# Opening weight units in places of their own, no split on GpSimd, and a reordered first norm, in a two-layer transformer block

## The chip, the cores and the metric

The kernel runs on one core of one Trainium2 chip. Its time is the device time of one execution in microseconds (us). Engines are named as in the profile: PE is TensorE's matmul, PEld its weight load, DVE VectorE, ACT ScalarE, POOL GpSimd, SP SyncE, which only issues DMAs here.

## The reference

The input is x (512 tokens, 1024 features), a context of 256 tokens, and vectors c and c_ctx that are turned into shifts, scales and gates (`w_mod`). Two layers follow, each of three sublayers, all of the form x + gate * f(modulate(rms_norm(x))):

```python
def modulate(x, g, shift, scale):
    return rms_norm(x, g) * (1.0 + scale) + shift
def macaron_half_ffn(x, g, shift, scale, gate, w_in, w_out):
    return x + 0.5 * gate * swiglu(modulate(x, g, shift, scale), w_in, w_out)
# layer 0: half FFN, even_mixer (neighbourhood attention + two-way mLSTM), half FFN
# layer 1: half FFN, spatial_gating, half FFN; then rms_norm(x, final_g)
```

In layer 0 the context goes through the first half FFN too, and feeds the mixer. An FFN is 1024 -> 2 x 2816 -> 1024. All is fp32.

## The kernel before, in words

Features lie on the partitions: x is `xT`, [128, 8, 512], the context `cT`, [128, 8, 256]. A product in fp32 accuracy is three matmuls of split operands: hi*hi, hi*lo, lo*hi (`product`; `product2` does x and context with the same weights). So each weight unit (512 KB, [128, 1024]) and each activation is split in two: ACT rounds it to `hi`, then a subtraction makes `lo = raw - hi`.

`Stream` (L61) brings the weights in one fixed order. `load` starts a DMA on SP into one of three `raw` places. `prep` splits a unit into the next of four `whi` and four `wlo` places (L81 to L84): the rounding on ACT (L83), the subtraction on DVE, or on GpSimd for the unit numbers in `W.pool` (L84). `next` hands a unit out, after splitting up to two units ahead of it and starting loads five ahead. A place of `whi` comes free when the last product with the unit in it is done. `W.pool` holds units 0 to 5, and for each of the five places in the stream where a sublayer begins (`mark`) the four units before and the four after it.

The sublayers are named by layer and number: 00 (FFN with context), 01 (mixer), 02 (FFN), 10 (FFN), 11 (gating), 12 (FFN). Each ends in `out_last` (L349): with its last four units, all held to the end, it forms the output first for tokens 0 to 255 and then for 256 to 511 (after 00 also for the context). Each of the eight products of such a part is followed by a residual on DVE (`xT`, L306), a square on ACT (`sq_x`) and an add on DVE (`nacc_x`, L230), which form the next norm's sum of squares. While the second part runs, the first part's norm is finished (`rstd`: matmul `st_x`, root on ACT, matmul `bc_x`) and DVE and ACT make the modulated input of the next sublayer, split in two (`nt_x` L255, `hx..h` L256, `hx..l` L257). The next sublayer then opens with products on tokens 0 to 255 alone, during which the second part's norm is finished. Its first four units, which hold the first weights, can be split only as `out_last` gives its four places free.

Order on each engine: a planner at build time runs through the program by its own costs, takes on each engine the ready instruction that the program names first, and so fixes each engine's queue; on the chip each engine keeps that order. Tiles whose places follow each other wait for each other's readers.

`Stage.open` (L376) reserves a sublayer's input `hx` (and `hc`) on the left side of SBUF. `gtiles` (L447) reserves the activations of an FFN, in 8 rotating places (6 with context); the last four (f 18 to 21) have places of their own, and small unused tiles (`spacer`, L44) shift some addresses by 64 or 192 bytes.

At the start of the program there is no sublayer before. x, the first modulation weights and the first weights are loaded by SP, interleaved by hand. `load_mod` (L566) loads a slice of 128 shift and 128 scale columns as four DMAs of 256 KB, whose runs are 512 bytes. `norm_start` (L589) squares on ACT, adds on DVE, and finishes the norm with matmuls (`sts`, `bcx`). `start` (L627) then goes over the eight feature blocks k: `x_products(k)` (matmuls `st`), `mod_columns(k+2)` and `mod_products(k+3)` (matmuls `pm`, a copy `mr` on DVE, matmuls `pcol`, from which DVE makes G and S of a block and then its input). The context's norm is started before block 4; its modulation and products (`stc`) follow at the end.

Of the kernel before, what the change touches and what calls it, by code (L numbers as in the profile page):

```python
# [8 lines left out]
F32 = mybir.dt.float32  # L9
F32R = mybir.dt.float32r  # L10
# [27 lines left out]
def block_kernel(ctx: ExitStack, tc: tile.TileContext, T: dict, out: bass.AP, stop: str = ""):  # L38
# [4 lines left out]
    def spacer(pool, n, name):  # L43

        nc.gpsimd.memset(pool.tile([P, n // 4], F32, name=name), 0.0)
# [15 lines left out]
    class Stream:  # L61
        def __init__(self):
            self.aps, self.raw, self.split = [], {}, {}
            self.nraw = self.nsplit = self.pos = 0
            self.pool = set()

        def load(self, upto):
# [8 lines left out]
        def prep(self, upto):  # L76
            while self.nsplit < min(upto, len(self.aps)):
                i = self.nsplit
                self.load(i + 1)
                r = self.raw.pop(i)  # L80
                hi = wp.tile(list(r.shape), F32R, tag="whi", name=f"whi{i}", bufs=4)  # L81
                lo = wp.tile(list(r.shape), F32R, tag="wlo", name=f"wlo{i}", bufs=4)
                nc.scalar.copy(hi, r)  # L83
                (nc.gpsimd if i in self.pool else nc.vector).tensor_tensor(lo, r, hi.bitcast(F32), ALU.subtract)  # L84
                self.split[i] = (hi, lo)
                self.nsplit += 1
# [262 lines left out]
    def out_last(nm, gs, gx, st, gc=None):  # L349

        u = [W.next() for _ in range(4)]
        warm(AF.Sqrt, gs[-1][1][:, 0:1].bitcast(F32))
        parts = [(xT, 0, t0, t1, gx, st.nx) for t0, t1 in HALVES]
        if gc is not None:
            parts.append((cTt[0], 2, 0, NCX, gc, st.nc))
        for x, g0, t0, t1, gg, nn in parts:
            for ot in range(KD):
                po = bank(f"pl{nm}{g0}{ot}{t0}")
                for e, g in enumerate(gs):
                    w = pick(u[ot // 2], slice(None), e, slice((ot % 2) * P, (ot % 2 + 1) * P))  # L360
                    product(po[:, :256], w, pick(g[g0:g0 + 2], slice(None), slice(t0, t1)), e == 0, e == len(gs) - 1)
                if ot in (1, 3):
                    st.go()
                residual(x, ot, t0, t1, po[:, :256], gg)
                nn.square(ot, t0, t1)
            st.feed(nn, t0, t1)


    class Stage:
# [7 lines left out]
        def open(self):  # L377
            self.stack = ExitStack()
            hp = self.stack.enter_context(tc.tile_pool(name=f"hp{self.name}", bufs=1, side=self.side, reuse_waits="tile"))
            if self.nc:  # L380
                spacer(hp, 64, f"padc{self.name}")
                self.hc = hpair(hp, NCX, f"hc{self.name}")
            spacer(hp, 64 if self.nc else 128, f"padx{self.name}")
            self.hx = hpair(hp, N, f"hx{self.name}")
            if self.name != "00":
                self.gx = gains(self.l, self.j, 0)
                self.gc = gains(self.l, self.j, 1) if self.nc else None

        def feed(self, nn, t0, t1):

# [7 lines left out]

        def close(self):
            self.stack.close()  # L400

    class Final:
        def __init__(self):
# [27 lines left out]
    def ffn(l, s, cur, nxt, gxf, gcf, bgsteps, side, first=None, left=0):  # L431
# [5 lines left out]
        with tc.tile_pool(name=f"g{nm}", bufs=1, side=side, reuse_waits="tile") as gp:  # L437
# [7 lines left out]
                    pace[0] = last  # L445

            def gtiles(f):  # L447
                e = f % nslot if hc or f < 18 else f"z{f}"
                if not hc and f == 18:
                    spacer(gp, 192, f"padz{nm}")  # L450
                g = [gp.tile([P, 512], F32R, tag=f"gx{e}{i}", name=f"gx{nm}{f}{i}") for i in range(2)]
                if hc:
                    if f < nslot:
                        spacer(gp, 192, f"padgc{f}")
                    g += [gp.tile([P, 256], F32R, tag=f"gc{e}{i}", name=f"gc{nm}{f}{i}") for i in range(2)]
                    if f < nslot:
                        spacer(gp, 64, f"padge{f}")
                if not hc and f == NF - 1:
                    spacer(gp, 64, f"padze{nm}")
                return g  # L460

            gs = {f: gtiles(f) for f in range(2)}
# [7 lines left out]
            for t0, t1 in () if first else HALVES:  # L470
                for f in range(2):
                    pab = bank(f"pa{nm}{f}{t0}"), bank(f"pb{nm}{f}{t0}")
                    for k in range(KD):
                        if (t0, f) == (0, 0) and k in (5, 7):
                            cur.go()
                        for ab in range(2):
                            w = pick(us[f][k // 4], slice(None), k % 4, slice(ab * P, (ab + 1) * P))
                            product(pab[ab][:, :256], w, pick(hx, slice(None), k, slice(t0, t1)), k == 0, k == 7)
                    glu(pab[0][:, :256], pab[1][:, :256], 256, gs[f][0][:, t0:t1], gs[f][1][:, t0:t1], f"{nm}{f}{t0}")
            bg.step(2 * bgsteps)  # L480
            for kind, f in ffn_order(l, s):
                if kind == "o":
# [64 lines left out]
    mark.append(len(W.aps))  # L547
    stream_ffn(1, 1)
    W.pool.update(range(6))
    for i in mark:  # L550
        W.pool.update(range(i - 4, i + 4))


    cpool = ExitStack()
# [12 lines left out]
    def load_mod(i):  # L567
        k0, k1 = MODK[i]
        t = sp.tile([P, KD, 2, (k1 - k0) * P], F32, tag="wmk", name=f"wmk{i}", bufs=5)
        for h in range(2):  # L570
            for j in range(2):
                nc.sync.dma_start(t[:, 4 * h:4 * h + 4, j], T["w_mod"][0, 512 * h:512 * h + 512, j * D + k0 * P:j * D + k1 * P]
                                  .rearrange("(k p) c -> p k c", p=P))
        wmk.append(t)

    for k in range(0, KD, 2):
# [9 lines left out]
        load_mod(i)  # L586
    warm(AF.Sqrt, cs[:, 0, 0:1])

    def norm_start(nn, n):  # L589
        st = aux(f"sts{n}")  # L590
        acc = sp.tile([P, N], F32, tag="sacc", name=f"sacc{n}", bufs=1)[:, :n]
        for k in range(KD):
            sq = sp.tile([P, N], F32, tag="ssq", name=f"ssq{n}{k}", bufs=4)[:, :n] if k else acc
            nc.scalar.activation(sq, nn.x[:, k], AF.Square)
            if k:
                nc.vector.tensor_tensor(acc, acc, sq, ALU.add)
        for c in range(n // P):
            mm(st[:, 2 * c:2 * c + 2], acc[:, c * P:(c + 1) * P], ones, True, True)
        r = tp.tile([P, 8], F32, tag="nrs", name=f"nrs{n}", bufs=1)[:, :n // 64]
        nc.scalar.activation(r, st[:, :n // 64], AF.Sqrt, bias=epst, scale=1.0 / D)  # L600
        if n == NCX:
            warm(AF.Silu, r[:, 0:1])
        nc.vector.reciprocal(r, r)
        bc = aux(f"bcx{n}")
        for c in range(n // P):
            mm(bc[:, c * P:(c + 1) * P], r[:, 2 * c:2 * c + 1].to_broadcast([P, P]), ident, True, True)
        return bc[:, :n]
# [12 lines left out]
    for k in range(5):  # L620
        mm(junk, ones[:, 0:1].to_broadcast([P, P]), xT[:, k], True, True)
    mrs = {0: mod_products(0)}
    bcx = norm_start(s00.nx, N)
    xn = sp.tile([P, KD, N], F32, name="xn")
    s00.open()

    def start():  # L627
# [52 lines left out]
        mod_columns(1, mrs[1])  # L680
        mrs[2] = mod_products(2)
        for k in range(KD):
            if k == 4:
                bc = norm_start(s00.nc, NCX)
            x_products(k)
            if k + 2 < KD:
                mod_columns(k + 2, mrs[k + 2])
            if k + 3 < KD:
                mrs[k + 3] = mod_products(k + 3)
# [109 lines left out]
    for cc in ((2, 3), (4, 5), (0, 1)):  # L799
        tok_block("vb0", 256, cc, ev_vb0, u01[0])  # L800
        tok_block("vb1", 272, cc, ev_vb1, u01[1])


    li = gt[:, :, 0]
# [417 lines left out]
    with tc.tile_pool(name="sgv", bufs=1, side="right", reuse_waits="tile") as vp:  # L1222
# [7 lines left out]
        for b in range(4):  # L1230
            pv = [bank(f"sv{b}{c}") for c in range(4)]
            us = [W.next() for _ in range(4)] if b == 0 else None
            for c0, c1 in ((0, 2), (2, 4)) if b == 0 else ((0, 4),):
                for i in range(4):
                    u = us[i] if b == 0 else W.next()
                    if b == c0 == 0 and i in (1, 2):
                        s11.go()
                    for c in range(c0, c1):
                        for kk in range(2):
                            k = 2 * i + kk  # L1240
                            product(pv[c], pick(hx, slice(None), k, slice(c * P, (c + 1) * P)), pick(u, slice(None), kk), k == 0, k == 7)
                for c in range(c0, c1):
                    nc.scalar.activation(halved(v[c][:, b * 512:(b + 1) * 512]), inorder(pv[c]), AF.Gelu_apprx_tanh)
        us = {}

        def ublock(b):
# [72 lines left out]
def layout(i):  # L1319
# [2 lines left out]
    a["cT"] = i["ctx"][0].T.reshape(KD, P, NCX).transpose(1, 0, 2)  # L1322
    a["cc"] = np.stack([i["c"][0], i["c_ctx"]]).reshape(2, KD, P).transpose(2, 0, 1)
    a["w_mod"] = i["w_mod"]
    a["b_mod"] = i["b_mod"].reshape(2, 9, KD, P).transpose(3, 0, 1, 2)
    a["norm_g"] = i["norm_g"].reshape(2, 3, KD, P).transpose(3, 0, 1, 2)
    a["final_g"] = i["final_g"].reshape(KD, P).T
# [74 lines left out]
```

## Time and profile before

| | |
|---|---|
| time, median of 3 runs (lowest to highest) | 2307.08 us (2306.27 to 2308.08) |
| the profiled execution's own time | 2307.41 us |
| its span, first to last instruction | 2305.6 us |
| PE busy | 2246.3 us (97%) |
| DVE busy | 1284.2 us (56%) |
| ACT busy | 779.7 us (34%) |
| POOL busy | 262.8 us (11%) |
| mean granted clock of TensorE | 0.985 |

A row of instructions has start, duration, engine, line, operation, output<-inputs with shapes, how many (x3), and in brackets the idle time of its engine just before it with what ended that. Matmuls overlap: their durations add up to more than the time they take. Where several like instructions are merged in a row, its duration is that of all of them together.

### The profile page before, as it was taken

Reading aid. Unit: us, or ns where it says so; the run is one execution under the profiler, and the core shown is the slowest. Engines: PE = TensorE matmul, PEld = TensorE weight load, DVE = VectorE, ACT = ScalarE, POOL = GpSimd, SP = SyncE. Lnnn points to the kernel's source line nnn. Section 1 sums busy time; section 2 is a strip of 40 time slices with the busy share of each in tenths; the row PEclk is TensorE's granted clock in tenths of the full one; section 3 lists DMA queues with packets and bytes.
Section 4 is the critical chain, followed back from the end, with each engine's and each line's share of the span. In section 5 each row is a group of like instructions: output and inputs, shape, how many; then the busy total and the mean of one; then the engine's idle time right before and its main releaser. Section 6 shows DMA issues by size and latency. Waiting matters only on the chain.

```text
span 2305.6 us, 31899 instructions
## 1 busy us (share of the span) xinstructions
PE 2246.3 (97%) x12926; PEld 1989.7 (86%) x12926; DVE 1284.2 (56%) x2045; ACT 779.7 (34%) x1283; POOL 262.8 (11%) x300
## 2 busy tenths in 40 slices
PE   7999999999999999999999999999999999999998
PEld 4999999999878977888888898888878888988887
DVE  5996653327556447766574766433536756433336
ACT  3322122124354356532323432322335424323222
POOL 2212120002030033100010301000300003000000
PEclk8999999999999989999999999999999999999999
DMA  8566561221122231165564356333242322333231
GB/s 268 175 201 196 167 185 65 70 68 52 63 83 65 65 119 62 65 210 192 173 211 155 111 174 210 101 101 101 92 146 93 99 92 74 101 100 108 94 110 65
DMA packets 95347, 281.33 MB, mean 122 GB/s; under 512 B 11024, under 2 KB 29632, under 8 KB 94816
## 3 DMA queue, kind: packets, MB, share of 16 engines
q1 hardware_dynamic: 69648, 196.18, 25.7%
q0 software_dynamic: 22960, 77.99, 11.3%
q10 hardware_dynamic: 2592, 5.13, 0.7%
q8 instruction: 101, 1.65, 0.3%
q14 instruction: 46, 0.38, 0.1%
HBM read 274.95 MB, written 6.00 MB: 122 GB/s over the span
## 4 chain that ended last, share of the span: by engine, by line
PE 88%; DVE 6%; issue 3%; ACT 1%; DMA 1%; POOL 0%; ACTq 0%; DVEq 0%; POOLq 0%
PE pa L108 19%; PE pb L108 19%; PE po L108 14%; PE pc L108 4%; PE su L108 4%; PE sv L108 4%; PE posg L108 3%; PE poc L108 2%; PE O L108 1%; PE tva L108 1%; PE nS L108 1%; PE st L108 1%; PE pomx L108 1%; PE fqa L108 1%; PE pl11l L108 1%
## 5 line engine op out<-in xcount | busy, mean ns | idle before, releaser
L83 ACT CAST whi<-raw 128x1024 fp32r<-128x1024 f32 x348 | 364.8, 1049 | 919.1 <-PE pb L108 330.4
L84 DVE TENSOR_TENSOR wlo<-raw,whi 128x1024 fp32r<-128x1024 f32 x302 | 370.1, 1226 | 399.6 <-ACT whi L83 383.7
L108 PE MATMUL po<-gx,whi 128*128 128x512 f32 x1024 | 305.4, 380 | 0.0
L441 DVE TENSOR_TENSOR sl<-sl,pb 128x512 f32<-128x512 f32 (+1 forms) x92 | 60.0, 652 | 272.0 <-PE pb L108 182.1
L108 PEld LDWEIGHTS po<-gx,whi 128*128 128x128 f32 x1024 | 183.7, 189 | 24.0
L108 PE MATMUL po<-gx,wlo 128*128 128x512 f32 x512 | 194.4, 380 | 0.0
L84 POOL TENSOR_TENSOR wlo<-raw,whi 128x1024 fp32r<-128x1024 f32 (+1 forms) x46 | 109.8, 2388 | 598.7 <-ACT whi L83 585.1
L161 DVE SCALAR_TENSOR_TENSOR macc<-wm,cs,macc 128x1024 f32<-128x1024 f32 x133 | 168.3, 1280 | 10.5 <-DMA wm<-in_w_mod 9.4
L153 POOL DMA_DIRECT2D wm<-in_w_mod x128 | 68.1, 532 | 573.9 <-DVE macc L161 368.7
L306 DVE SCALAR_TENSOR_TENSOR xT<-po,gate,xT 128x512 f32<-128x512 f32 x80 | 59.8, 748 | 95.9 <-PE po L108 95.8
L440 ACT ACTIVATE sl<-pa 128x512 f32<-128x512 f32 (+1 forms) x92 | 52.3, 569 | 174.3 <-PE pa L108 174.3
L108 PEld LDWEIGHTS po<-gx,wlo 128*128 128x128 f32 x512 | 97.2, 190 | 10.2
L108 PE MATMUL pc<-hc00l,whi 128*128 128x256 f32 x320 | 88.0, 275 | 0.0
L108 PE MATMUL pc<-hc00h,whi 128*128 128x256 f32 x320 | 87.3, 273 | 0.0
L108 PE MATMUL pc<-hc00h,wlo 128*128 128x256 f32 x320 | 87.2, 273 | 0.0
L108 PE MATMUL pa<-hx12l,whi 128*128 128x512 f32 (+1 forms) x192 | 70.5, 367 | 3.1 <-DVE hx12l L257 3.1
L108 PE MATMUL pa<-hx10l,whi 128*128 128x512 f32 (+1 forms) x192 | 70.2, 366 | 3.1 <-DVE hx10l L257 3.1
L108 PE MATMUL pa<-hx02l,whi 128*128 128x512 f32 (+1 forms) x192 | 70.2, 366 | 2.8 <-DVE hx02l L257 2.8
L108 PE MATMUL pa<-hx02h,whi 128*128 128x512 f32 (+1 forms) x192 | 70.3, 366 | 0.1
L108 PE MATMUL pa<-hx12h,whi 128*128 128x512 f32 (+1 forms) x192 | 70.3, 366 | 0.0
L108 PE MATMUL pa<-hx10h,whi 128*128 128x512 f32 (+1 forms) x192 | 70.1, 365 | 0.0
L108 PE MATMUL pa<-hx12h,wlo 128*128 128x512 f32 (+1 forms) x192 | 70.0, 365 | 0.0
(561 smaller groups left out, 5893.6 us busy)
## 6 DMA issues: line engine op xcount, KB each, us to landing
raw<-in_ffn_in SPq DMA_DIRECT2D x176, 512.0 KB, 3.3
wm<-in_w_mod POOLq DMA_DIRECT2D x128, 512.0 KB, 4.6
raw<-in_ffn_out SPq DMA_DIRECT2D x64, 512.0 KB, 3.3
raw<-in_mix_in SPq DMA_DIRECT2D x26, 512.0 KB, 3.2
wmk<-in_w_mod SPq DMA_DIRECT2D x32, 256.0 KB, 5.4
raw<-in_ffn_last SPq DMA_DIRECT2D x16, 512.0 KB, 3.3
raw<-in_sg_v SPq DMA_DIRECT2D x16, 512.0 KB, 3.4
raw<-in_sg_u SPq DMA_DIRECT2D x16, 512.0 KB, 3.5
```

The source lines that it names most:

```text
L83: nc.scalar.copy(hi, r)
L84: (nc.gpsimd if i in self.pool else nc.vector).tensor_tensor(lo, r, hi.bitcast(F32), ALU.subtract)
L108: lastmm[0] = nc.tensor.matmul(o, lhsT, rhs, start=start, stop=stop)
L153: ins = nc.gpsimd.dma_start(wt, T["w_mod"][l, k * P:(k + 1) * P, j * D:(j + 1) * D])
L161: nc.vector.scalar_tensor_tensor(acc[v], wt, cs[:, v, k:k + 1], acc[v], ALU.mult, ALU.add)
L306: nc.vector.scalar_tensor_tensor(xs, inorder(o), g[:, k:k + 1], xs, ALU.mult, ALU.add)
L440: nc.scalar.activation(halved(sl), inorder(pa), AF.Silu)
L441: nc.vector.tensor_tensor(halved(sl), halved(sl), inorder(pb), ALU.mult)
```

## The change

Units that open a sublayer get tiles of their own in a pool that `Stage.open` opens on the same side as `hx`: none for 01, two for 02, four for 10 and 11, one for 12. `out_last` calls `W.prep` for them right after it has taken its own four units. The pool is closed when the opening products have been issued. Units around the marks leave `W.pool`, so DVE does their subtraction; units 0 to 5 stay on GpSimd. The own places of f 18 to 21 and all spacers in `gtiles` go. At the start, the modulation weights of layer 0 come from an input laid out so that a slice is two DMAs of 512 KB with runs of 4 KB. The context's squares are issued two by two after blocks 3 to 6, their adds go to GpSimd, and the norm's matmuls follow block 6.

```diff
@@ Stream.prep
-                hi = wp.tile(list(r.shape), F32R, tag="whi", name=f"whi{i}", bufs=4)
-                lo = wp.tile(list(r.shape), F32R, tag="wlo", name=f"wlo{i}", bufs=4)
+                if i in self.ahead:
+                    hi, lo = (self.ahead[i].tile(list(r.shape), F32R, name=f"w{p}{i}") for p in ("hi", "lo"))
+                else:
+                    hi = wp.tile(list(r.shape), F32R, tag="whi", name=f"whi{i}", bufs=4)
+                    lo = wp.tile(list(r.shape), F32R, tag="wlo", name=f"wlo{i}", bufs=4)
@@ out_last
         u = [W.next() for _ in range(4)]
+        if isinstance(st, Stage):
+            W.prep(st.upto)
@@ Stage.open
+                self.first = ExitStack()
+                m = mark[NAMES.index(self.name)]
+                self.upto = m + AHEAD[self.name]
+                if self.upto > m:
+                    fp = self.first.enter_context(tc.tile_pool(name=f"wf{self.name}", bufs=1, side=self.side, reuse_waits="tile"))
+                    W.ahead.update({i: fp for i in range(m, self.upto)})
+    NAMES = ("01", "02", "10", "11", "12")
+    AHEAD = {"01": 0, "02": 2, "10": 4, "11": 4, "12": 1}
@@ gtiles
-                e = f % nslot if hc or f < 18 else f"z{f}"
-                if not hc and f == 18:
-                    spacer(gp, 192, f"padz{nm}")
+                e = f % nslot
...
-                        spacer(gp, 192, f"padgc{f}")
...
-                        spacer(gp, 64, f"padge{f}")
-                if not hc and f == NF - 1:
-                    spacer(gp, 64, f"padze{nm}")
@@ after the opening products of an FFN (and likewise in 01 and 11)
+            if not first:
+                cur.first.close()
@@ W.pool
     W.pool.update(range(6))
-    for i in mark:
-        W.pool.update(range(i - 4, i + 4))
@@ load_mod
-            for j in range(2):
-                nc.sync.dma_start(t[:, 4 * h:4 * h + 4, j], T["w_mod"][0, 512 * h:512 * h + 512, j * D + k0 * P:j * D + k1 * P]
-                                  .rearrange("(k p) c -> p k c", p=P))
+            nc.sync.dma_start(t[:, 4 * h:4 * h + 4], T["w_mod0"][k0, h])
@@ norm_start
+    def square_start(nn, n, k, eng):
+        if k == 0:
+            sacc[n] = sp.tile([P, N], F32, tag="sacc", name=f"sacc{n}", bufs=1)[:, :n]
+        sq = sp.tile([P, N], F32, tag="ssq", name=f"ssq{n}{k}", bufs=4)[:, :n] if k else sacc[n]
+        nc.scalar.activation(sq, nn.x[:, k], AF.Square)
+        if k:
+            eng.tensor_tensor(sacc[n], sacc[n], sq, ALU.add)
@@ start (for x: square_start on nc.vector for all k, then norm_start(N))
         for k in range(KD):
-            if k == 4:
-                bc = norm_start(s00.nc, NCX)
             x_products(k)
+            if 3 <= k < 7:
+                for i in range(2 * k - 6, 2 * k - 4):
+                    square_start(s00.nc, NCX, i, nc.gpsimd)
+            if k == 6:
+                bc = norm_start(NCX)
@@ layout
+    a["w_mod0"] = i["w_mod"][0, :, :2 * D].reshape(2, 4, P, 2, KD, P).transpose(4, 0, 2, 1, 3, 5)
```

## Rows read from the trace of the kernel before

**Rows 1.** The page: busy time by engine, and shares of the last chain.

```profile
PE 2246.3 (97%) x12926; PEld 1989.7 (86%) x12926; DVE 1284.2 (56%) x2045; ACT 779.7 (34%) x1283; POOL 262.8 (11%) x300
...
PE 88%; DVE 6%; issue 3%; ACT 1%; DMA 1%; POOL 0%; ACTq 0%; DVEq 0%; POOLq 0%
```

**Rows 2.** PE's waits: for whom, us in total, how often, the longest.

```profile
PE st_x L108 <- DVE nacc_x L230: 12.2, 5, 4.2
...
PE pa L108 <- DVE hx10l L257: 3.1, 3, 1.3
PE pa L108 <- DVE hx12l L257: 3.1, 3, 1.2
...
PE pa L108 <- DVE hx02l L257: 2.8, 3, 1.2
PE pcol L108 <- DVE mr L616: 2.7, 1, 2.7
...
PE st_c L108 <- DVE nacc_c L230: 2.1, 1, 2.1
PE tvb L108 <- DVE cT L306: 2.0, 1, 2.0
...
PE sv L108 <- ACT hx11h L256: 1.1, 1, 1.1
PE sv L108 <- DVE hx11l L257: 0.9, 1, 0.9
```

**Rows 3.** DVE in order of time, where 02 ends and 10 begins.

```profile
1303.62 2.23 DVE L230 TENSOR_TENSOR nacc_x<-nacc_x,sq_x 128x256 f32<-128x256 f32 x1
...
1308.70 4.72 DVE L257 SCALAR_TENSOR_TENSOR hx10l<-nt_x,mod,hx10h 128x256 fp32r<-128x256 f32 x3
...
1314.86 1.26 DVE L257 SCALAR_TENSOR_TENSOR hx10l<-nt_x,mod,hx10h 128x256 fp32r<-128x256 f32 x3
```

**Rows 4.** POOL in the same stretch.

```profile
1303.20 2.38 POOL L84 TENSOR_TENSOR wlo<-raw,whi 128x1024 fp32r<-128x1024 f32 x1 [11.14 <-ACT whi L83]
1307.78 2.39 POOL L84 TENSOR_TENSOR wlo<-raw,whi 128x1024 fp32r<-128x1024 f32 x1 [2.20 <-ACT whi L83]
```

**Rows 5.** Stretches: length, busy by engine, clock; last the six at boundaries.

```profile
16.00:26.24 10.24, 8.95 (x37) 4.87 (x40) 6.24 (x16) 1.75 (x2) 4.59 (x2) 0.50 1.06 334
43.31:50.13 6.82, 5.76 (x26) 3.13 (x27) 2.79 (x11) 0.81 (x1) 0.00 (x0) 0.50 0.66 256
...
sum 30.71, PE 28.39 PEld 27.40 DVE 8.19 ACT 12.24 POOL 2.37; mean PE 4.73 PEld 4.57 DVE 1.37 ACT 2.04 POOL 0.39
```

**Rows 6.** Groups by line: the subtractions, count | busy, mean ns | idle before.

```profile
L84 DVE TENSOR_TENSOR wlo<-raw,whi 128x1024 fp32r<-128x1024 f32 x302 | 370.1, 1226 | 399.6 <-ACT whi L83 383.7
...
L84 POOL TENSOR_TENSOR wlo<-raw,whi 128x1024 fp32r<-128x1024 f32 (+1 forms) x46 | 109.8, 2388 | 598.7 <-ACT whi L83 585.1 <-DVE mod L176 8.1 <-DVE xT L306 3.2
```

**Rows 7.** Stretch of `out_last` ahead of 11: PE, PEld, DVE, ACT, POOL.

```profile
1642.50:1664.90 22.40, 22.40 (x202) 22.37 (x201) 14.83 (x28) 10.27 (x20) 7.57 (x4) 1.00 0.19 68
```

**Rows 8.** DVE and POOL at the context's first norm, in order of time.

```profile
38.45 5.25 DVE L596 TENSOR_TENSOR sacc<-sacc,ssq 128x256 f32<-128x256 f32 x7 [0.87 <-ACT ssq L594]
...
37.87 2.37 POOL L84 TENSOR_TENSOR wlo<-raw,whi 128x1024 fp32r<-128x1024 f32 x1 [1.88 <-ACT whi L83]
```

**Rows 9.** DMA packets in 16 to 20 us, and in 12 to 14 us.

```profile
DMA packets 2758, 1.37 MB, mean 343 GB/s; under 512 B 82, under 2 KB 2758, under 8 KB 2758
...
DMA packets 359, 0.84 MB, mean 422 GB/s; under 512 B 27, under 2 KB 171, under 8 KB 359
```

**Rows 10.** Matmuls by tile: duration ns least/median/most, first and last start.

```profile
L108 PE MATMUL pl01l<-gx,wlo x64: 275/275/276, 1288.8 to 1310.8; 128*128 128x256 f32 x64
...
L108 PE MATMUL pl00l<-gx,wlo x64: 275/275/276, 535.7 to 557.7; 128*128 128x256 f32 x64
...
L108 PE MATMUL fqa<-hx01h,wlo x32: 388/389/397, 814.0 to 835.1; 128*128 128x512 f32 x32
...
L108 PE MATMUL fqb<-hx01h,wlo x32: 379/379/379, 635.9 to 693.8; 128*128 128x512 f32 x32
```

More of the change, by code (lines that the diff above doesn't have):

```diff
@@ L64, in __init__ @@
             self.nraw = self.nsplit = self.pos = 0
+            self.ahead = {}
             self.pool = set()
@@ L447, in gtiles @@
             def gtiles(f):
-                e = f % nslot if hc or f < 18 else f"z{f}"
-                if not hc and f == 18:
-                    spacer(gp, 192, f"padz{nm}")
+                e = f % nslot
                 g = [gp.tile([P, 512], F32R, tag=f"gx{e}{i}", name=f"gx{nm}{f}{i}") for i in range(2)]
                 if hc:
-                    if f < nslot:
-                        spacer(gp, 192, f"padgc{f}")
                     g += [gp.tile([P, 256], F32R, tag=f"gc{e}{i}", name=f"gc{nm}{f}{i}") for i in range(2)]
-                    if f < nslot:
-                        spacer(gp, 64, f"padge{f}")
-                if not hc and f == NF - 1:
-                    spacer(gp, 64, f"padze{nm}")
                 return g
@@ L587, in block_kernel, with norm_start @@
     warm(AF.Sqrt, cs[:, 0, 0:1])
-    def norm_start(nn, n):
-        st = aux(f"sts{n}")
[L591 to L596, printed above, removed]
+    sacc = {}
+    def square_start(nn, n, k, eng):
[5 more added lines that the diff above has]
+            eng.tensor_tensor(sacc[n], sacc[n], sq, ALU.add)
+    def norm_start(n):
+        st = aux(f"sts{n}")
+        acc = sacc[n]
         for c in range(n // P):
@@ L622, in block_kernel @@
     mrs = {0: mod_products(0)}
-    bcx = norm_start(s00.nx, N)
+    for k in range(KD):
+        square_start(s00.nx, N, k, nc.vector)
+    bcx = norm_start(N)
     xn = sp.tile([P, KD, N], F32, name="xn")
@@ L801, in block_kernel @@
         tok_block("vb1", 272, cc, ev_vb1, u01[1])
+    s01.first.close()
     li = gt[:, :, 0]
@@ L1243, in block_kernel @@
                     nc.scalar.activation(halved(v[c][:, b * 512:(b + 1) * 512]), inorder(pv[c]), AF.Gelu_apprx_tanh)
+        s11.first.close()
         us = {}
```

## The prediction

> **What bounds the kernel now.** I read the page first. PE is busy for 97% of the span and makes 88% of the last chain [rows 1], so only time in which PE waits, or runs at the lower clock, can go; the matmuls themselves stay. Second, the waits of PE alone. Outside the start, two thirds of them sit where one sublayer ends and the next opens: `st_x`, which wants the second part's sum of squares, 12.2 us over the five boundaries (4.2 at one, so 2.0 at each other); the opening products on `hx10l`, `hx12l` and `hx02l`, 3.1, 3.1 and 2.8; and in 01 and 11 `st_c` 2.1, `tvb` 2.0, `sv` 1.1 and 0.9 [rows 2]. That is 27.3 us, and all but one row wait for DVE.
>
> Third, what DVE does there. In the stretch from 02 to 10 the reader sees a `nacc_x` add of 2.23 us and three `hx10l` of 4.72 us together, and further down three others of the same shape in 1.26 [rows 3]. The slow ones lie on top of a subtraction on POOL, 1303.20 to 1305.58 and from 1307.78 on [rows 4]: the add ends 0.27 us after POOL does. So a DVE operation with two SBUF inputs that meets a POOL subtraction is held until POOL is through. The rows show two of the four subtractions that POOL has in the last part and the opening there; all five boundaries are alike in this.
>
> Fourth, the clock by stretches. After these waits the granted clock is 0.50, the lower level of 1.2 GHz, in six stretches of 30.71 us, in which PE is busy for 28.39 [rows 5]. At 2.4 GHz that work would take half, so they cost 14.2 us. Waits and clock at the five boundaries make 41.5 us of the 2305.6.
>
> The start has one such place of its own: the context's seven adds hold DVE for 5.25 us, the first behind a POOL subtraction [rows 8]; the copy `mr` stands behind them in DVE's queue, PE waits 2.7 us for it [rows 2], and then runs 5.76 us at the lower clock [rows 5], another 2.9.
>
> **The change part by part.**
>
> *No subtraction on GpSimd around the marks.* Of POOL's 46, six (units 0 to 5) stay, so 40 go, eight per boundary. On DVE one takes 1.226 us instead of 2.388 [rows 6]. The two rows of 4.72 and 2.23 us are 5.3 us longer than like work (1.26 for three `hx10l`; the add I put at 0.42, a third of that), and the fourth subtraction meets another one, which I put at 0.7: about 6 us of DVE's time per boundary, from end to end on the path. In exchange DVE gets 8 x 1.226 = 9.8 us of work per boundary. What hides it is the room before the norm is due: in the 22.4 us of `out_last`, DVE is busy for 14.83, of which some 5 are being held, so about 12.6 are free [rows 7]. 9.8 fit, if they come early.
>
> *Own places for the opening units.* That is what makes them early. For 10 and 11 all four opening units are split as soon as `out_last` begins, since they wait for no `whi` place. For 02 two, and for 12 three, still wait for a place that comes free in the second part, 1.226 us each on DVE, 2.5 and 3.7 us against the 6 that go. The planner now prices this work on DVE, where before it did not price the holding, so it puts `st_x` behind more opening products. The added wait: a tile above `hx` waits for the last reader of that memory. At 02 this is the attention's tiles, read to the end before `out_last`; at 10, 11 and 12 long-finished units. Behind it on DVE and ACT would stand the residuals, which have six PSUM banks to lag in; I cost it at nothing. After the ahead units the next two (m+4, m+5) find places early, in the second part, and may take 2.5 us of DVE at the wrong time: kept as a remainder below.
>
> Of the four boundaries with own places, the waits are 27.3 less 01's 6.1 (2.0 of `st_x`, 2.1, 2.0), so 21.2. Their clock is 14.2 less 01's share; 01 has two of the six stretches, which I put at a third, 4.7, so 9.5. Of 30.7 I leave 1.5 each at 02 and 12 and 0.8 each at 10 and 11, 4.6 in all: **26.1 us** gained. Bounds: nothing (if latency sets the end anyway) and 30.7.
>
> *01 has no place ahead.* Its four subtractions stay late and turn from POOL to DVE, 4 x 1.226 = 4.9 us against four holdings of about 2 each, 8. The relief is 3 in 8, more where the planner now moves `st_c` back. Of 10.8 (6.1 and 4.7) I take half: **5.4 us**; bounds 0 and 10.8.
>
> *The context's first norm.* DVE loses the 5.25 us, so `mr` no longer waits: 2.7 and the 2.9 of clock, **5.6 us**. The price is seven POOL adds of 128x256; by the POOL row a quarter of 2.39 each, 0.6, in all 4.2 us in which DVE can be held [rows 4]. The nearest evidence that this hurts is that same holding; but PE has products of blocks 3 to 7 to go on with, and DVE has idle time between blocks, so I take 0 of it and keep 4.2 as the bound.
>
> *The relaid modulation weights.* Eight slices of 1 MB, 8.39 MB, come in 512-byte packets at 343 GB/s in a stretch that holds little else; where mostly 4 KB packets run it is 422 [rows 9]. 24.5 against 19.9 us: the stream ends 4.6 us earlier, and SP issues 16 DMAs instead of 32, with the loads of units 2 and 3 and the context behind them on its queue moving up too. PE waits for slices only now and then and the first products wait also for the norm, so I take half, **2.3 us**; bounds 0 and 4.6. The Trainium skill, "DMA: Bandwidth & Descriptors", Specifications, says that transfers reach line rate from 512 bytes up; by that the new layout gains nothing and the sum is 2.3 us smaller. The rows here show a fifth more rate at 4 KB, so I keep the term.
>
> *Spacers and own places of f 18 to 21.* The tile of f 18 now takes the place of f 10, whose last reader, the second output group, is done before f 16 begins; no wait. Addresses shift by 192 bytes. Tiles shifted so and not shifted run alike now, 275 ns for `pl01l` and `pl00l` [rows 10], so 0. Bound: the block whose input is read in another order takes 389 against 379 ns [rows 10]. At 10 ns per 512 columns, 00 (384 matmuls each of `po` and `poc`, some 380 smaller ones of `out_c` and `out_last`) and the three other `out_last` would lose about 11 us. A faster reading is excluded, as all are at the same least value. The dropped POOL memsets are nothing.
>
> Sum: 26.1 + 5.4 + 5.6 + 2.3 = 39.4 us. The profiled execution took 2307.41, 1.8 more than its span, which stay. 2307.41 - 39.4 = 2268.0; it stands 0.3 above the median of the runs, so **2267.7 us**.
>
> **The rivals.**
>
> *Latency, not holding, sets the boundary.* From the last residual to `st_x` runs a chain of DVE, ACT, DVE that no freed engine shortens; and the late DVE splits of m+4 and m+5 fall into it. For it: those two units do get their places exactly then. Against: three rows of waits are on `hx..l`, which needs no late residual [rows 2]. Half of 31.5 stays: 2283.5.
>
> *All of it goes, and the clock holds.* 41.5 at the boundaries, 5.6 and 4.6 at the start, 51.7: 2255.4. The early low stretch, 8.95 us of PE at half clock [rows 5], could give up to 4.5 more, 2250.9. For it: the planner can hide what is left behind 10 us of opening products. Against: 01, 02 and 12 keep late units.
>
> *The start gives nothing,* the POOL adds holding DVE for as long as it is spared (4.2 against 5.25): 2307.1 - 31.5 = 2275.6.
>
> *The spacers mattered:* 11 us back, 2278.7.
>
> *Slower: DVE becomes the bound of each boundary.* If the eight splits don't fit ahead, each stands before a residual in DVE's queue, and PE, out of banks, stops in `out_last` too. 40 x 1.226 = 49 us come onto the path and about 6 x 4 + 8 = 32 go: 17 slower, with nothing from the start 2324. It decides from DVE's free time in `out_last`: above 9.8 us it does not happen, and the row leaves about 12.6.
>
> **How the numbers follow.** The forecast 0.55, latency 0.15, all of it 0.13, nothing from the start 0.07, spacers 0.06, slower 0.04. The likeliest gives 2267.7, with a range of its own of 2258 to 2278. Ends of all bounds without the slower rival lie near 2251 and 2290; I take 2248 to 2290, which leaves out the slower case and the edges of the latency case and of the full gain, about one in eight. A difference of 0.2% (4.6 us) is about what a measurement of this kernel tells from no change. Faster 0.94, same 0.02, slower 0.04.
>
> **What would show it.** In the changed profile POOL's `wlo` count is 6; no `hx..l` or `nacc_x` at a boundary takes over 0.6 us; PE's wait for `st_x` falls from 12.2 to under 4, and the `pa` rows on `hx..l` nearly vanish; the clock stays at 1.00 at 968, 1323, 1675 and 1951 but may drop at 565 to 589. In the start the wait of `pcol` on `mr` is gone and the first `pa` comes some 8 us earlier than now. I am wrong if DVE at the boundaries is busy without a gap through the opening products, if `po` of 00 is over 379 to 383 ns, or if the waits turn to `whi` or `wlo`.

## The result, and the profile after

| | before | after |
|---|---|---|
| time, median (lowest to highest), 4 runs each | 2307.16 us (2306.27 to 2308.08) | 2277.27 us (2276.84 to 2279.05) |
| ratio, with its 95% interval | | 0.9872 [0.9855, 0.9889] |
| the profiled execution's own time, its span | 2307.41, 2305.6 | 2279.05, 2277.2 |
| mean granted clock of TensorE | 0.985 | 0.991 |

29.9 us are gone, where 39.4 were forecast. The time lies in the range, 9.6 us above the forecast. That hides two misses of opposite sign, and the waits of PE after the change show both. The columns are engine, tile and line, whom it waited for, us in total, how often, the longest.

```profile
PE pa L112 <- DVE wlo L88: 5.4, 2, 5.2
...
PE st L112 <- ACT hx00h L649: 3.1, 3, 1.3
PE st_x L112 <- DVE nacc_x L234: 2.7, 6, 0.8
...
PE plmx L112 <- ACT y L1183: 1.4, 1, 1.4
...
PE sv L112 <- ACT hx11h L260: 1.1, 1, 1.1
PE pa L112 <- ACT hx02h L260: 0.9, 1, 0.9
PE pa L112 <- ACT hx10h L260: 0.9, 1, 0.9
...
PE pcol L112 <- DVE mr L626: 0.5, 1, 0.5
```

Against [rows 2]: `st_x` fell from 12.2 to 2.7, all `pa` rows on `hx..l` and the rows of `st_c` and `tvb` are gone, and what is left at the boundaries (2.7, 1.4, 1.1, 0.9, 0.9) makes 7.0 us of 27.3. The first row is new: one wait of 5.2 us for a `wlo`. It stands just behind the start, and in the clock by stretches (length, then busy time of PE, PEld, DVE, ACT and POOL, then the granted clock) it is followed by a low stretch that the kernel before had not; the openings of 02, 10, 11 and 12, which were at 0.50 [rows 5], run at 1.00:

```profile
94.23:101.05 6.82, 6.07 (x19) 5.25 (x20) 6.82 (x9) 1.38 (x3) 0.82 (x2) 0.50 0.78 269
...
955.00:980.00 25.00, 23.82 (x201) 23.21 (x201) 18.31 (x40) 14.96 (x29) 0.00 (x0) 1.00 0.26 85
1305.00:1330.00 25.00, 23.73 (x201) 23.13 (x200) 17.22 (x40) 13.37 (x27) 0.00 (x0) 1.00 0.20 64
1653.00:1680.00 27.00, 25.66 (x121) 21.82 (x120) 15.10 (x34) 11.01 (x23) 0.00 (x0) 1.00 0.39 125
1920.00:1945.00 25.00, 24.85 (x214) 24.32 (x213) 20.80 (x45) 14.22 (x31) 0.00 (x0) 1.00 0.26 84
```

So the boundaries gave nearly all they had, and the start, instead of giving 7.9 us, lost 5.2 us and half of 6.07, some 8 us, just behind it.

### The profile page after: what moved, and what is told of

Read it like the earlier page. It is cut to its first block, busy times and chain, and to the rows that moved or that the text cites. A ratio compares the mean times of both kernels' runs of the same rounds, so it can differ in the third digit from the quotient of the medians.

```text
span 2277.2 us, 31825 instructions
## 1 busy us (share of the span) xinstructions
PE 2234.8 (98%) x12926; PEld 1978.3 (87%) x12926; DVE 1289.1 (57%) x2078; ACT 782.3 (34%) x1287; POOL 172.6 (8%) x249
## 4 chain that ended last, share of the span: by engine, by line
PE 87%; DVE 5%; issue 4%; ACT 2%; DMA 1%; POOL 0%; DVEq 0%; ACTq 0%; POOLq 0%
PE pa L112 19%; PE pb L112 19%; PE po L112 14%; PE pc L112 4%; PE su L112 4%; PE sv L112 3%; PE posg L112 3%; PE poc L112 2%; PE O L112 1%; PE tva L112 1%; PE nS L112 1%; PE S L112 1%; PE pomx L112 1%; PE fqa L112 1%; PE pl11l L112 1%
## 5 line engine op out<-in xcount | busy, mean ns | idle before, releaser
L88 DVE TENSOR_TENSOR wlo<-raw,whi 128x1024 fp32r<-128x1024 f32 x342 | 421.7, 1235 | 407.1 <-ACT whi L87 389.7
L112 PE MATMUL pa<-hx02h,wlo 128*128 128x512 f32 (+1 forms) x192 | 69.5, 362 | 0.0
L112 PE MATMUL pb<-hx02l,whi 128*128 128x512 f32 (+1 forms) x192 | 69.5, 362 | 0.0
L112 PE MATMUL pa<-hx10h,wlo 128*128 128x512 f32 (+1 forms) x192 | 69.5, 362 | 0.0
L112 PE MATMUL pb<-hx10l,whi 128*128 128x512 f32 (+1 forms) x192 | 69.5, 362 | 0.0
```

Source lines behind the costliest of these rows:

```text
L112: lastmm[0] = nc.tensor.matmul(o, lhsT, rhs, start=start, stop=stop)
```

## The experiments: the boundaries

The theory: GpSimd's subtractions hold DVE's operations, and that is the boundary loss. Its rivals: the splits were late, and own places make them early; or the length of the GpSimd subtraction itself was on the path.

**One edit: `W.pool`.**

```diff
     W.pool.update(range(6))
-    for i in mark:
-        W.pool.update(range(i - 4, i + 4))
```

> The kernel before with one edit: W.pool holds units 0 to 5 alone, so 40 subtractions move from GpSimd to DVE; no own places, start as before. Theory A (the holding of DVE was the whole boundary loss, and late splits on DVE cost little): the 41.5 us of waits and half clock go but for 1 to 2 us a boundary, so 2307 - 33 = about 2274, no DVE operation at a boundary stretched. Theory B (own places are needed: without them four splits a boundary come late, 4 x 1.23 us each): about half goes, as I took for 01, so 2307 - 17 = about 2290, with waits of the opening products on wlo in all five boundaries.

Measured: 2269.52 us (5 runs), before in the same series 2306.92, ratio 0.9842 [0.9822, 0.9862]. So 37.4 us from this edit alone, and 7.8 us below the whole change. PE's waits have no row for `st_x` at all; `wlo` is waited for once, in 11. The stretches round all five boundaries run at a clock of 1.00. Theory A. The two longest waits left at the boundaries:

```profile
PE sv L108 <- DVE wlo L84: 1.2, 1, 1.2
PE sv L108 <- ACT hx11h L256: 1.1, 1, 1.1
```

**The boundary parts together**, with own places (the start as before). The spacers and the places of f 18 to 21 go too; the diff is shortened.

```diff
+                if i in self.ahead:
+                    hi, lo = (self.ahead[i].tile(list(r.shape), F32R, name=f"w{p}{i}") for p in ("hi", "lo"))
...
+        if isinstance(st, Stage):
+            W.prep(st.upto)
...
-    for i in mark:
-        W.pool.update(range(i - 4, i + 4))
```

> The changed kernel's boundary parts alone: own places, no split on GpSimd round the marks, no spacers in gtiles (own places for f 18 to 21 don't fit beside them and go too); the start is that of the kernel before. Theory A (the boundaries gave some 38 us and the new start takes some 8 back): about 2307 - 38 = 2269, and no wait of pa for wlo at 89 to 95 us. Theory B (the start is worth its 2 us or more, and the wait at 89 to 95 us comes from the boundary parts): about 2277 + 2 = 2280, with that wait.

Measured: 2271.63 us (4 runs), ratio 0.9845 [0.9826, 0.9864]; of the wait for `wlo` after the start 0.2 us are left. 35.3 us; the own places add nothing to the edit of `W.pool` (2.1 us slower, the intervals overlap). Theory A.

**Own places alone**, the splits left on GpSimd: the same diff without its last two lines (the spacers gone here too).

> The changed kernel's own places alone, with the splits round the marks left on GpSimd and the start of before (the spacers in gtiles and the places of f 18 to 21 go too, for room). Theory A (GpSimd's holding of DVE is the whole boundary loss; places are worth nothing): the holdings only move, so 2300 to 2310, with DVE operations at the boundaries still stretched to 2 us and more and most of the 12.2 us of st_x left. Theory B (early splits are worth half of the gain, by places or by engine alike): about 2290.

Measured: 2305.52 us (11 runs) against 2306.80, ratio 0.9996 [0.9987, 1.0004]: no difference. PE's waits in this run:

```profile
PE st_x L112 <- DVE nacc_x L234: 17.4, 7, 5.7
...
PE pa L112 <- DVE hx12l L261: 2.7, 3, 1.6
```

With the splits early but on GpSimd, `st_x` waits longer than before (17.4 against 12.2): the holding has only moved. Theory A.

**GpSimd made to run for nothing.** In the first experiment's kernel GpSimd does the subtraction of the four units before and the four after each mark (`idle`) again, into scratch. The spacers and the places of f 18 to 21 are left out, for room.

```diff
                 (nc.gpsimd if i in self.pool else nc.vector).tensor_tensor(lo, r, hi.bitcast(F32), ALU.subtract)
+                if i in self.idle:
...
+                    for q in range(4):
+                        scr = wp.tile([P, 256], F32, tag="scr", name=f"scr{i}{q}", bufs=1)
+                        nc.gpsimd.tensor_tensor(scr, r2[:, 256 * q:256 * q + 256], h2[:, 256 * q:256 * q + 256], ALU.subtract)
```

> e1_pool_only (2269.5; here without the spacers in gtiles and the places of f 18 to 21, for room) in which GpSimd does the subtractions of the units round the marks a second time, in four pieces each, into a scratch tile that nobody reads; DVE still makes the wlo that PE uses. So nothing waits for GpSimd, and only its running beside DVE is put back. Theory A (GpSimd's subtraction holds DVE, and that was the boundary loss): stretched nacc and hx..l again, st_x waits of 2 us and more back, most of 37 us lost again: 2295 to 2310. Theory B (it was the subtraction's length or its place in a queue, on the way to wlo): 2270 to 2272.

Measured: 2303.16 us (11 runs) against 2306.95, ratio 0.9981 [0.9972, 0.999]. 33.6 of the 37.4 us are lost again, though no instruction of PE, ACT or DVE reads these copies. Groups of DVE and POOL by line (count, then busy us, mean ns of one), first of the kernel before, then of the first experiment, then of this one:

```profile
L230 DVE TENSOR_TENSOR nacc_x<-nacc_x,sq_x 128x256 f32<-128x256 f32 x70 | 38.6, 551 | 20.7 <-ACT sq_x L229 19.9
L257 DVE SCALAR_TENSOR_TENSOR hx10l<-nt_x,mod,hx10h 128x256 fp32r<-128x256 f32 x16 | 11.2, 736 | 0.0
```

```profile
L230 DVE TENSOR_TENSOR nacc_x<-nacc_x,sq_x 128x256 f32<-128x256 f32 x70 | 29.4, 419 | 16.7 <-ACT sq_x L229 16.6
...
L257 DVE SCALAR_TENSOR_TENSOR hx10l<-nt_x,mod,hx10h 128x256 fp32r<-128x256 f32 x16 | 6.9, 476 | 0.0
```

```profile
L236 DVE TENSOR_TENSOR nacc_x<-nacc_x,sq_x 128x256 f32<-128x256 f32 x70 | 37.0, 528 | 16.8 <-ACT sq_x L235 16.6
...
L263 DVE SCALAR_TENSOR_TENSOR hx10l<-nt_x,mod,hx10h 128x256 fp32r<-128x256 f32 x16 | 9.8, 658 | 0.0
...
L90 POOL TENSOR_TENSOR scr<-raw,whi 128x256 f32<-128x256 f32 x160 | 150.1, 938 | 740.8 <-ACT whi L84 624.9 <-issue 103.8 <-POOL padx L45 0.9
```

The reader is to see 551, 419, 528 and 736, 476, 658: the same additions and subtractions, longer in both kernels where GpSimd runs beside them. The copy is not exact: it runs for 150.1 us in shorter pieces, DVE keeps its own `wlo` beside it and makes some of them slower, and `raw` is kept longer. So the waits come back in other places than I expected. `st_x` waits only 0.8 us, not 2 at each boundary; the rest is on residuals (`xT`), on `hx..l` and `hx..h`, and on one `wlo` in 11, which is likely of the copy's own making:

```profile
PE sv L114 <- DVE wlo L85: 5.0, 1, 5.0
PE pb L114 <- DVE xT L312: 4.9, 3, 2.1
...
PE st_x L114 <- DVE nacc_x L236: 0.8, 1, 0.8
```

The time is theory A's. The run shows the cause, not its size to the us.

**Where the time went.** The start takes a different time in each profile, also where nothing in it was edited: in the five with the old start the first `stc` begins at 62.40 to 67.11 us. So profiles are better compared from there. The stretch to the first `plmx` (the first product of `out_last` in 01) holds the boundary into 01, the one from there to the first `pq11c` (in 12) the other four:

| kernel | `stc` to `plmx`, us | `plmx` to `pq11c`, us |
|---|---|---|
| before | 861.70 | 1336.26 |
| `W.pool` alone | 851.84 | 1308.87 |
| boundary parts, with own places | 852.13 | 1311.48 |
| own places alone | 860.14 | 1335.87 |
| GpSimd for nothing | 857.06 | 1335.09 |
| the whole change | 860.79 | 1311.54 |

`W.pool` alone gives 9.9 us at 01 and 27.4 at the other four; GpSimd working for nothing takes back 5.2 and 26.2 of them.

## The experiments: the start

**The start alone.**

```diff
+            nc.sync.dma_start(t[:, 4 * h:4 * h + 4], T["w_mod0"][k0, h])
...
-            if k == 4:
-                bc = norm_start(s00.nc, NCX)
             x_products(k)
+            if 3 <= k < 7:
+                for i in range(2 * k - 6, 2 * k - 4):
+                    square_start(s00.nc, NCX, i, nc.gpsimd)
+            if k == 6:
+                bc = norm_start(NCX)
```

> The changed kernel's start alone: relaid modulation weights, context's squares two by two with GpSimd adds, norm after block 6; boundaries and GpSimd splits as before. Theory A: first pa 2 to 3 us earlier, then a wait of 4 to 6 us for wlo and a stretch at half clock behind it before 110 us: about 2307 + 6 = 2313. Theory B (the start gains as predicted): 2307 - 8 = 2299 and no such wait.

Measured: 2309.53 us (12 runs) against 2306.92, ratio 1.0011 [1.0002, 1.002]. It gains nothing, and costs 2.6 us. The first `pa` starts at 71.11 us instead of 75.37, and then PE waits 3.8 us for `msum` at 102.8 and falls to 0.50. One pair of profiles does not price the earlier `pa`: over the five profiles with the old start it lies at 73.12 to 77.82, over the five with the whole new one at 71.11 to 73.00, by the medians 3.8 us earlier. Theory A in kind, at half its size, with `msum` in the place of `wlo`.

```profile
PE mt L108 <- DVE msum L167: 3.8, 1, 3.8
```

**Is it the place of the split in DVE's queue?** The changed kernel with:

```diff
+            if first:
+                W.prep(W.pos + 4)
             bg.step(2 * bgsteps)
```

> The changed kernel with one line more: before the background's first steps after the start (12 steps of the next modulations) the program splits units 6 and 7 (W.prep(W.pos + 4)), so that in DVE's queue both subtractions stand ahead of all but one of the sums macc. Theory A (the wait at 89 to 95 us is the place of the subtraction in the queue, 5.2 us and 3.4 us of half clock): 2277 - 8 = about 2269, no wlo wait and full clock at 94 to 101. Theory B (the raw loads or the place of whi are what is late, or the sums and their paced loads give the time back later): 2275 to 2279.

Measured: 2277.56 us (4 runs), ratio 0.9869 [0.9851, 0.9888], as the change. My theory A falls: the wait for `wlo` is gone (0.2 us are left), but it has become another.

```profile
PE mt L112 <- DVE msum L171: 6.2, 2, 3.8
```

Whatever stands first on DVE, something that stands behind is late. In the profile of the change DVE is idle before all of this, and the row names what for (start, length, and in brackets the idle time before and what ended it):

```profile
72.34 1.51 DVE L458 TENSOR_TENSOR gx<-slst,gx 128x512 fp32r<-128x512 f32 x1 [0.68 <-ACT gx L457]
77.88 0.76 DVE L163 TENSOR_SCALAR macc<-wm,cs 128x1024 f32<-128x1024 f32 x1 [4.03 <-DMA wm<-in_w_mod]
...
82.94 10.85 DVE L165 SCALAR_TENSOR_TENSOR macc<-wm,cs,macc 128x1024 f32<-128x1024 f32 x9
93.70 2.36 DVE L88 TENSOR_TENSOR wlo<-raw,whi 128x1024 fp32r<-128x1024 f32 x2
```

`wm`, the weights of the next modulations, is loaded from GpSimd's queue. There, before and after the change:

```profile
61.08 1.08 POOL L153 DMA_DIRECT2D wm<-in_w_mod  x2 [2.30 <-DVE sttc L643]
70.60 5.16 POOL L84 TENSOR_TENSOR wlo<-raw,whi 128x1024 fp32r<-128x1024 f32 x2 [8.45 <-ACT whi L83]
75.71 0.73 POOL L153 DMA_DIRECT2D wm<-in_w_mod  x1
```

```profile
40.20 5.96 POOL L602 TENSOR_TENSOR sacc<-sacc,ssq 128x256 f32<-128x256 f32 x7
68.40 4.90 POOL L88 TENSOR_TENSOR wlo<-raw,whi 128x1024 fp32r<-128x1024 f32 x2 [22.24 <-ACT whi L87]
73.26 1.60 POOL L157 DMA_DIRECT2D wm<-in_w_mod  x3
```

Before, two loads leave at 61.08, ahead of the subtractions of units 4 and 5; after, these stand in front, wait 22.24 us for their rounded halves, and the first load leaves at 73.26. The second theory: the queue on GpSimd has turned, and DVE's sums start late. Three runs try it.

**The context's norm alone**: the diff of the start without its first line.

> The kernel before with the context's first norm reordered alone (squares two by two, adds on GpSimd, norm after block 6), modulation weights in the old layout. Theory A (this edit puts the two subtractions of units 4 and 5 ahead of the first wm loads in GpSimd's queue, and so makes the new wait): pcol no longer waits 2.7 us for mr, the wm loads leave some 10 us later than before, PE then waits 3 to 4 us for msum or wlo near 100 us, with half clock behind it: 2307 + 3 to + 6 = 2310 to 2313. Theory B (the gain of 5.6 us as predicted): 2301 to 2302.

Measured: 2309.15 us (12 runs) against 2306.80, ratio 1.0008 [0.9999, 1.0016]: no gain. The wait on `mr` is 0.5 instead of 2.7; `mt` waits 3.6 for `msum` (from 104.9 us on), and the queue is the turned one, so this edit by itself turns it:

```profile
68.49 4.91 POOL L84 TENSOR_TENSOR wlo<-raw,whi 128x1024 fp32r<-128x1024 f32 x2 [22.24 <-ACT whi L83]
73.58 1.60 POOL L153 DMA_DIRECT2D wm<-in_w_mod  x3
```

**Units 4 and 5 off GpSimd.** The changed kernel with one number changed:

```diff
-    W.pool.update(range(6))
+    W.pool.update(range(4))
```

> The changed kernel with one number changed: W.pool holds units 0 to 3 in place of 0 to 5, so that the first wm loads stand behind no subtraction in GpSimd's queue. Theory A (the loss of 8 us after the start is the late wm loads, behind the subtractions of units 4 and 5, which wait for the end of the first products): wm loads leave before 66 us, DVE begins macc some 4 us earlier, no wait of over 2 us for wlo or msum before 110 us, 2277 - 8 = about 2269. Theory B (DVE has simply too much to do there, wherever the loads stand): two more subtractions on DVE, 2277 to 2280.

Measured: 2272.60 us (4 runs), ratio 0.9848 [0.9832, 0.9863]: 4 to 5 us better than the change. The loads leave at 55.54, the wait for `wlo` falls from 5.4 to 0.2, and the clock holds in the stretch that was low:

```profile
55.54 1.59 POOL L157 DMA_DIRECT2D wm<-in_w_mod  x3 [10.83 <-ACT hx00h L649]
```

```profile
94.23:101.05 6.82, 6.82 (x44) 6.26 (x43) 6.82 (x7) 1.64 (x2) 1.06 (x2) 1.00 0.61 166
```

Theory A, for about half of its 8 us. The rest seems to stay on DVE, which is busy for all of these 6.82 us: `mt` waits 1.2 for `msum`, and `poc` 1.4 for a product of DVE's just before 337 us. Even so the new start is worth nothing beside the old one: the boundary parts alone took 2271.63.

**The relaid weights**: the first line of the start's diff, on top of the edit of `W.pool` alone.

> e1_pool_only (2269.5) with the modulation weights relaid. By my term of 2.3 us (half of 4.6): about 2267, first pa 2 us earlier than in e1 and no new wait, as GpSimd's queue has two wm loads ahead of the subtractions, as before. Rival (512-byte packets are not what limits the start): 2269 to 2270. Second rival (the whole 4.6): 2265.

Measured: 2268.77 us (4 runs) against 2306.80, ratio 0.9831 [0.9816, 0.9847]; without them 0.9842 [0.9822, 0.9862]. By the medians that is some 0.7 us, by the ratios 2.5; the intervals tell it neither from nothing nor from my 2.3, though the stretch from 16 to 20 us has a fifth more rate. Beside the reordered norm they gain nothing (2309.53 with them, 2309.15 without, 12 runs each). Without and with, on `W.pool` alone:

```profile
DMA packets 2783, 1.38 MB, mean 346 GB/s; under 512 B 82, under 2 KB 2783, under 8 KB 2783
```

```profile
DMA packets 460, 1.67 MB, mean 418 GB/s; under 512 B 52, under 2 KB 52, under 8 KB 460
```

## The experiments: versions that beat both

The edit of `W.pool` with units 4 and 5 on DVE and the whole new start, without own places (the diff is shortened):

```diff
-    W.pool.update(range(6))
-    for i in mark:
-        W.pool.update(range(i - 4, i + 4))
+    W.pool.update(range(4))
...
+            nc.sync.dma_start(t[:, 4 * h:4 * h + 4], T["w_mod0"][k0, h])
...
+            if k == 6:
+                bc = norm_start(NCX)
```

> A version made of what helped: no split on GpSimd round the marks, units 4 and 5 on DVE too (W.pool holds 0 to 3), relaid weights, reordered context norm; no own places, spacers as before. From e7 (2268.8) and the start of e8 (excess of PE's spacing up to 150 us 14.4 against 15.6 in e7): 2266 to 2268. Rival (the start's order costs what it gives, as in e8 the sums behind it): 2269 to 2272.

Measured: 2270.70 us (5 runs) against 2306.95, ratio 0.985 [0.9836, 0.9863]: the rival. The reordered norm does not pay here either; `poc` waits 1.5 just before 339 us and a low stretch follows. The times do not tell this run from the one with units 4 and 5 on DVE (2272.60, ratio 0.9848), but the stretch from `plmx` to `pq11c` does: it takes 1308.87 to 1308.90 us in the four kernels with the edit of `W.pool` and without own places, and 1311.26 to 1311.54 in the four with them. So own places, with the spacers gone in the same kernels, cost about 2.5 us there.

The same without the reordered norm:

> e7 (2268.8) with units 4 and 5 split on DVE and the context's norm left as before. If the two subtractions on GpSimd hold DVE at the end of the first products (5.16 us for two, gx stretched to 1.51 us), about 1 us less: 2267 to 2268. If they are hidden: 2269; if DVE is too full before 110 us: 2271 to 2274.

Measured: 2268.92 us (4 runs, 2266.27 to 2275.52), ratio 0.9842 [0.9827, 0.9857]: not told from the kernel with units 4 and 5 on GpSimd, and too wide to tell my three cases apart. So with the norm left as it was, no gain of moving these two is seen, and the queue is in order without it. The best median is that of the kernel with two edits, `W.pool` and the relaid weights, at 2268.77, 8.5 us below the change; the plain edit of `W.pool` is as good within the intervals.

## Why the prediction was right in its time and wrong in its parts

| step | forecast, us | measured, us | from |
|---|---|---|---|
| five boundaries | 26.1 + 5.4 = 31.5 | 35.3; without own places 37.4 | parts alone, `W.pool` alone |
| context's first norm | 5.6 | -2.4, not told from 0 | norm alone |
| relaid weights | 2.3 | 0.7 by medians, not told from 0 or 2.3 | with and without, on `W.pool` |
| the start beside the boundary parts | 7.9 | -5.6 | 2271.63 against 2277.27 |
| spacers and places of f 18 to 21 | 0 | none seen; not tried alone | `po` 379 ns at least and in the median, before and after |

The boundaries gave 3.8 us more than forecast, the start 13.5 less. That the time still fell into the range is in part luck: the first miss covers some of the second.

*No subtraction on GpSimd: right, and under-sized.* That a DVE operation with two SBUF inputs waits out a GpSimd subtraction was the cause, and the edit of `W.pool` and the run with GpSimd working for nothing show it. After the change no `nacc_x` or `hx..l` takes over 0.49 us. The Trainium skill, "SBUF — State Buffer", Who interferes with whom, says that such an instruction contends with a GpSimd one that reads SBUF. The trace agrees, and shows the limit too: `nt_x`, which reads one input from SBUF and one from PSUM, takes at most 482 ns in the same stretches in which `hx10l` takes up to 2661, though two of the three `nt_x` in the last row here run beside the subtraction that began at 1307.78 [rows 4].

```profile
L255 DVE SCALAR_TENSOR_TENSOR nt_x<-xT,G,bc_x x80: 466/472/482, 552.7 to 1963.0; 128x256 f32<-128x256 f32 x80
...
L257 DVE SCALAR_TENSOR_TENSOR hx10l<-nt_x,mod,hx10h x16: 471/476/2661, 1308.7 to 1332.7; 128x256 fp32r<-128x256 f32 x16
...
1307.53 1.26 DVE L255 SCALAR_TENSOR_TENSOR nt_x<-xT,G,bc_x 128x256 f32<-128x256 f32 x3
```

I left 4.6 us at four boundaries and half of 10.8 at 01; in the run of `W.pool` alone only 1.2 and 1.1 us of waits in 11 remain. The four boundaries came out near the forecast, 27.4 us against 26.1; the term that was too small is 01's, 9.9 against 5.4. There I netted four late splits against four holdings. They don't weigh alike: no wait for `wlo` appears at 01, while the holdings stood in the chain to `st_x`.

*Own places: the step failed.* I wrote of them "That is what makes them early", and eight splits were to fit only if they come early. Without them the only wait for `wlo` at a boundary is the 1.2 us in 11, so DVE's free time in `out_last`, which I put at 12.6 us [rows 7], was enough; alone they give nothing, and beside the other edit they cost about 2.5 us. The slower rival, DVE as the bound, stayed away for the same reason. The waits show where the cost lies: in the kernel with the boundary parts `st_x` waits 2.3 us in five waits and `pa` 0.9 each for `hx02h` and `hx10h`, none of which the run of `W.pool` alone has; it has the 1.2 for `wlo` instead. Why the norm comes later there, these runs don't show.

*The context's first norm: the gain came, and was taken back.* The wait of `mr` fell to 0.5 us and the low stretch after it went, and the first `stc` starts at 59.99 to 61.97 us in the six profiles with the reordered norm, at 62.33 to 67.11 in the seven without. I priced the seven GpSimd adds as holding DVE, and asked nothing else of GpSimd's queue. What failed there: the `wm` loads issued from that queue now stand behind two subtractions that start only at 68.40 us. Moving these two off GpSimd gave back 4.7 of the 5.6 us that the start lost. Which half of the edit turns it, the adds or the later place, was not tried.

*The relaid weights: the term stays open.* The rate rose as the rows had it; in the run without them PE waits 0.4 us in all for these slices (`wmk`). By the Trainium skill's rule of 512 bytes ("DMA: Bandwidth & Descriptors", Specifications) the term was nothing: for the rate the trace contradicts it, 346 against 418 GB/s; in the time, on `W.pool` alone, the runs tell neither nothing nor my 2.3 us from what came.

*What should have shown it.* POOL's `wlo` count is 6 and the low stretches of the four boundaries are gone, as said. The first `pa` came 2.4 us earlier in this pair of profiles and not 8, and "the waits turn to `whi` or `wlo`" was the sign that I was wrong: it was there, behind the start.

## What to carry to other kernels

Where a GpSimd operation runs beside a chain of DVE operations that each read two SBUF tiles, count what it holds, not only what it takes off DVE: here moving 40 subtractions of 1.2 us to the busier engine made the kernel 37 us faster. When work is moved, read every queue that it passes for the DMAs issued from it, and ask what comes to stand in front of them; a gain of some 4 us at one place was more than paid back 30 us later, as the loads left 12 us later. And try the single edits of a change by themselves: one of this one was better than the whole.

## What the runs showed of the hardware

Seven GpSimd adds of 128x256 took 5.96 us, one every 0.85, where I had put a quarter of a 128x1024 subtraction, 0.6; in pieces of 256 columns the subtraction too took 788 ns a piece in the median (938 in the mean, DVE running beside it) against 2388 for 1024 [rows 6]. The adds held DVE little: beside them a `hx00l` took 1.03 us instead of 0.69, and one operation each of `stt` and `G` 0.5 more, 1.3 us together.

A DVE operation with one SBUF tile can be held as well. Of the 19 products that open a sum `macc` in the kernel before, one took 2.87 us instead of 0.75; it began near 73.5 us, while GpSimd subtracted from 70.60 to 75.76. I had thought of two inputs only; the section of the Trainium skill named above counts `tensor_scalar` among what can contend, under conditions on its operands, and this row agrees.

```profile
L159 DVE TENSOR_SCALAR macc<-wm,cs x19: 714/746/2865, 73.5 to 1414.5; 128x1024 f32<-128x1024 f32 x19
```
